# End of the experts: first products of the next model between the last loads, and a padded third tile in retention

## The chip, the core and the metric

One core of a Trainium2 chip runs the whole program in one launch. Its engines work side by side, each on its own list of instructions, strictly in the order of the list: TensorE (PE; the loading of its weights is shown as PEld), VectorE (DVE), ScalarE (ACT), GpSimd (POOL), and SyncE (SP), which here only issues loads and stores. An instruction that has to wait for another engine holds up everything behind it in its list. The metric is the time of one execution in microseconds.

## What is computed

Two small transformer models in a row, on 256 tokens and 16 meta tokens (272 columns), width 1024, float32. The first has one layer: a mixer, then 32 experts in four groups, of which each token uses two. Its output passes a norm and is the input of the second model, whose first layer is retention: four heads, each with q, k, v and a gate from one projection.

```python
u = rmsnorm(h, norm_ffn_g[l]).reshape(b * t, d)
h = h + hier_moe(u, ...).reshape(b, t, d)          # 32 experts, silu(x w1) * (x w3) @ w2
return rmsnorm(h, norm_final_g)[:, N_META:]        # input of the second model
...
proj = hn @ w_in                                   # hn = rmsnorm of it, 1024 -> 6144
q = apply_rope(q, cos, sin); k = apply_rope(k, cos, sin) * (DK ** -0.5) * valid
sc = einsum(q, k) * decay; o = einsum(sc, v)       # per head, by chunks of 64
on = (o - mean) * rsqrt(var + GN_EPS) * gn_g
return (silu(gate) * on) @ w_o
```

## The kernel before

**Wide products.** A weight of the second model is split into a high part (wh, on ScalarE) and a low part (wl, on VectorE), and the input likewise into U's two halves. Each tile of 128 x 128 makes three products of 272 columns (lines 313, 314 and 315). A *block* is 128 outputs; over the 1024 inputs it takes 8 tiles, 24 products. One split covers 8 tiles, one load of 1 MB 16 tiles. A split of a weight writes one of three pairs of buffers; a load goes to one of three buffers named raw.

**Experts.** The 32 experts are done in 8 rounds of 4; a round `g` takes 24 loads of 1 MB (16 for w1 and w3, 8 for w2), 192 in all. I count them from 0 to 191; the last round has 168 to 191, the last eight of which are its w2, in two halves `z` of four. `expert_fetch` issues them on SP (line 1079), into 13 buffers in turn: 3 raw, 6 raw2, 4 raw3. At load 182 it first issues the second model's first load (`second_fetch`, line 1075), which takes a raw buffer too. After the four loads of one half z, ScalarE copies the result (`y`, line 1046), TensorE spreads it back to the tokens (line 1050) and VectorE adds it to the residual `h` (line 1052). `enter` then makes U of h, eight parts of 128 rows in all.

**The handover.** The first four blocks of retention's projection are computed in two steps, because U's second half is ready only after the last load: `begin_first` does inputs 0 to 511 of all four blocks (48 products) just ahead of the last load's products, and `begin_rest` the other 48 behind the last `y`. The input's norm factor isn't known yet: products are made of the input without it, and the factor `row` is multiplied in afterwards (`enter_norms`, two steps, lines 1204 to 1217: a chain of small operations on VectorE, then a product that spreads it over 128 rows, line 1214). retention multiplies the rotary tables by row (`cr`, `sr`, lines 1307 and 1308) and the first four blocks by these (`ro`, lines 1327 to 1331); GpSimd makes q and k of them (`rq`, `rk`, lines 1332 and 1333). Only then is an accumulator free for block 4.

**Retention.** `rot` makes q and k, and the generator `attention` does a head's scores and outputs in steps, one in the middle of each block of the wide products. The 272 keys are tiles of 128, 128 and 16; products with the third tile have 16 columns of weights (scores, line 1347, and transposes, line 1357) or 16 rows (line 1369). `spread` copies a norm factor to all rows; for 272 columns its third product has 16 rows too (line 440).

What decides the order: the lists are made by a scheduler from the order in which the code is written and from what each instruction waits for, so that an instruction can come earlier than the code has it.

Of the kernel before, what the change touches and what calls it, by code (L numbers as in the profile page):

```python
# [16 lines left out]
P = 128  # L17
# [256 lines left out]
class Kern:  # L274
# [58 lines left out]
    def begin_first(self, ws, nkb, cut, xh, xl, cols, then=None, at=()):  # L333
        ps = [self.acc() for _ in range(3)] + [self.att()]
        for i, (p, (c0, n)) in enumerate(zip(ps, cols)):
            self.tiles(ws, p, range(cut), nkb, xh, xl, c0, n)
            if i in at:
                next(then, None)
        self.begun = list(zip(ps, cols))

    def begin_rest(self, ws, nkb, cut, xh, xl, then=None, at=()):
# [500 lines left out]
    def moe(self):  # L842
# [4 lines left out]
        with ExitStack() as ctx:  # L847
# [150 lines left out]
            for g in range(8):  # L998
# [35 lines left out]
                for z in range(2):  # L1034
                    p = self.att()
                    for f in range(4):
                        if g % 2 and j < 3:
                            gather(j + 1, 4 * z + f)
                        if g == 7 and z == 1 and f == 3:
                            self.begin_first(self.ws, KB, 4, self.u2[:, 0], self.u2[:, 1], [(0, T)] * 4)  # L1040
                        w = self.expert_chunk()
                        for e in range(4):
                            mm(p[32 * e:32 * e + 32], ht[:, f * P + e * 32:f * P + e * 32 + 32],  # L1043
                               w[:, 512 * e:512 * e + 512], start=f == 0, stop=f == 3)
                    y = wk.tile([P, 512], F32, name="y")
                    act(y, p, AF.Copy)
                    for b in (0, 2):
# [126 lines left out]
    def enter_start(self):  # L1174
        self.u2 = self.glob.tile([P, 2, KB, T], F32R, name="U")
        self.nc.vector.tensor_copy(self.h[:, :, :NM], self.meta)
        self.split(self.u2[:, 0, :, :NM], self.u2[:, 1, :, :NM], self.meta_t)

# [20 lines left out]
    def enter_norms(self, r1):  # L1199
# [16 lines left out]
        dve.tensor_copy(self.row[:, NM:], p[:, 256:])  # L1216
        dve.tensor_copy(r1, p[:, :256])
# [75 lines left out]
    def retention(self, u):  # L1293
# [4 lines left out]
        with self.tc.tile_pool(name="ret", bufs=1, reuse_waits="tile") as m, \  # L1298
# [6 lines left out]
            cr = m.tile([P, T], F32, name="cr")  # L1305
            sr = m.tile([P, T], F32, name="sr")
            dve.tensor_mul(cr, self.c("c2"), r)
            dve.tensor_mul(sr, self.c("s2"), r)
# [14 lines left out]
            def rot(name):  # L1323
                o = w.tile([P, 2, T], F32, name=name)
# [244 lines left out]
```

## Time and profile before

| | us |
|---|---|
| time, median of 3 runs | 1493.98 (1493.14 to 1494.16) |
| the profiled execution | 1488.68 |
| its span, first to last instruction | 1487.0 |
| TensorE busy in it | 1317.5 (89%) |
| VectorE, ScalarE, GpSimd busy | 722.1, 522.0, 124.4 |
| mean granted clock of TensorE | 0.929 |

The profiled execution is one run, 5.3 us shorter than the median of the others. All rows of the trace are of it, and its times count from the start of the span. A row of busy times is a stretch; in a row of single instructions the first number is its start and the second its length, and "x8" says how many were merged. The text in square brackets is the idle time ahead of it, and what ended it.

### The profile page before, as it was taken

How to read it: one execution, taken by the hardware profiler on the slowest of the kernel's cores; microseconds unless marked ns; L12 is line 12 of the kernel's file. 1: busy time of each engine (PE TensorE's matmuls, PEld its weight loads, DVE VectorE, ACT ScalarE, POOL GpSimd, SP SyncE). 2: the span in 40 equal slices, each digit the busy share in tenths (PEclk: the TensorE clock that was granted, in tenths of full speed). 3: DMA queues.
4: the chain of work that ended last, by engine and by line, in shares of the span. 5: the costliest groups of instructions: out<-in, count | busy, mean ns of one | idle time of the engine just before them, and what ended most of it. 6: DMA issues, size and time to landing. Idle time of an engine off the chain costs nothing.

```text
span 1487.0 us, 23794 instructions
## 1 busy us (share of the span) xinstructions
PE 1317.5 (89%) x9750; PEld 1048.3 (71%) x9750; DVE 722.1 (49%) x1419; ACT 522.0 (35%) x895; POOL 124.4 (8%) x153
## 2 busy tenths in 40 slices
PE   7999997775777667768999999999999999999997
PEld 7898994220221212104899999999999999899996
DVE  7866684110100101002766665766666865766654
ACT  5466651000000000002333443544444554554442
POOL 4010020000000000000122111100000211100001
PEclk9999999887777878769999999999999999999998
DMA  8443677999999999998334334445555433355551
GB/s 309 133 127 112 217 261 300 425 426 425 426 426 426 426 427 426 427 396 359 117 138 143 127 133 155 153 172 171 173 176 184 165 114 124 132 188 183 197 193 63
DMA packets 55553, 359.54 MB, mean 242 GB/s; under 512 B 6416, under 2 KB 7056, under 8 KB 16144
## 3 DMA queue, kind: packets, MB, share of 16 engines
q1 hardware_dynamic: 55440, 357.97, 63.4%
q8 instruction: 78, 1.28, 0.3%
q14 instruction: 35, 0.29, 0.1%
HBM read 356.90 MB, written 1.05 MB: 241 GB/s over the span
## 4 chain that ended last, share of the span: by engine, by line
PE 49%; DMA 22%; DVE 3%; ACT 1%; issue 1%; POOL 0%; SPq 0%; DVEq 0%; ACTq 0%; POOLq 0%
DMA raw<-in_wm 22%; PE acc L313 14%; PE acc L315 14%; PE acc L314 14%; DVE wl L301 1%; ACT wh L300 1%; PE att L440 1%; PE att L1550 0%; PE att L1367 0%; PE att L1343 0%; DVE U L305 0%; PE att L409 0%; PE att L1043 0%; PE att L1369 0%; PE att L1460 0%
## 5 line engine op out<-in xcount | busy, mean ns | idle before, releaser
L313 PE MATMUL acc<-U,wh 128*128 128x272 f32 (+1 forms) x1456 | 423.2, 291 | 11.6 <-ACT U L304 9.2
L314 PE MATMUL acc<-U,wl 128*128 128x272 f32 (+1 forms) x1456 | 416.3, 286 | 1.4 <-DVE wl L301 1.4
L315 PE MATMUL acc<-U,wh 128*128 128x272 f32 (+1 forms) x1456 | 416.6, 287 | 0.4 <-DVE U L305 0.4
L301 DVE TENSOR_TENSOR wl<-raw,wh 128x1024 fp32r<-128x1024 f32 x232 | 285.3, 1230 | 187.3 <-ACT wh L300 186.8
L300 ACT ACTIVATE wh<-raw 128x1024 fp32r<-128x1024 f32 x232 | 245.6, 1060 | 325.2 <-PE acc L315 209.9
L313 PEld LDWEIGHTS acc<-U,wh 128*128 128x128 f32 x1456 | 275.7, 189 | 17.6 <-ACT U L304 10.2
L314 PEld LDWEIGHTS acc<-U,wl 128*128 128x128 f32 x1456 | 276.0, 190 | 2.6 <-DVE wl L301 1.6
L315 PEld LDWEIGHTS acc<-U,wh 128*128 128x128 f32 x1456 | 275.4, 189 | 2.8 <-DVE h L1052 0.8
L1012 PE MATMUL acc<-raw,U 128*32 128x512 f32 x1024 | 185.9, 822 | 86.5 <-DMA raw<-in_wm 81.3
L1012 PEld LDWEIGHTS acc<-raw,U 128*32 128x32 f32 x1024 | 25.0, 124 | 229.8 <-DMA raw<-in_wm 205.2
L1026 DVE TENSOR_TENSOR hid<-hid,acc 128x512 f32<-128x512 f32 x8 | 5.5, 688 | 218.0 <-PE acc L1012 218.0
L315 PE MATMUL acc<-hl,wh 128*128 128x272 f32 (+1 forms) x352 | 99.4, 283 | 0.0
L314 PE MATMUL acc<-hh,wl 128*128 128x272 f32 (+1 forms) x352 | 99.3, 282 | 0.0
L313 PE MATMUL acc<-hh,wh 128*128 128x272 f32 (+1 forms) x352 | 99.1, 281 | 0.0
L1043 PE MATMUL att<-raw,ht 128*32 128x512 f32 x512 | 74.5, 680 | 23.6 <-DMA raw<-in_wm 19.4
L301 DVE TENSOR_TENSOR wl<-rawh,wh 128x512 fp32r<-128x512 f32 x112 | 81.0, 757 | 17.9 <-ACT wh L300 17.8
L1052 DVE TENSOR_TENSOR h<-h,att 128x512 f32<-128x512 f32 x32 | 22.0, 688 | 129.7 <-PE att L1050 129.7
L300 ACT ACTIVATE wh<-rawh 128x512 fp32r<-128x512 f32 x112 | 65.0, 624 | 33.8 <-PE acc L315 20.4
L313 PEld LDWEIGHTS acc<-hh,wh 128*128 128x128 f32 x352 | 66.3, 188 | 0.0
L315 PEld LDWEIGHTS acc<-hl,wh 128*128 128x128 f32 x352 | 66.2, 188 | 0.0
L314 PEld LDWEIGHTS acc<-hh,wl 128*128 128x128 f32 x352 | 66.1, 188 | 0.0
L313 PE MATMUL acc<-yh,wh 128*128 128x272 f32 (+1 forms) x192 | 56.7, 295 | 3.2 <-DVE h L362 3.2
(387 smaller groups left out, 1832.7 us busy)
## 6 DMA issues: line engine op xcount, KB each, us to landing
raw<-in_wm SPq DMA_DIRECT2D x192, 1024.0 KB, 19.6
raw<-in_ws SPq DMA_DIRECT2D x114, 1024.0 KB, 4.9
rawh<-in_ws SPq DMA_DIRECT2D x56, 512.0 KB, 4.0
raw<-in_ws SPq DMA_DIRECT2D x4, 512.0 KB, 18.5
const<-in_const SPq DMA_DIRECT2D x1, 1056.0 KB, 15.3
out<-Q SPq DMA_DIRECT2D x4, 256.0 KB, 2.5
h<-in_xt SPq DMA_DIRECT2D x2, 272.0 KB, 4.8
h<-in_xt SPq DMA_DIRECT2D x1, 544.0 KB, 7.4
```

What stands on the lines that cost most here:

```text
L300: self.nc.scalar.activation(hi, src, AF.Copy)
L301: self.nc.vector.tensor_sub(lo, src, hi.bitcast(F32))
L313: mm(p[:, :n], wh, xh[:, kb, c0:c0 + n], start=kb == first, stop=False)
L314: mm(p[:, :n], wl, xh[:, kb, c0:c0 + n], start=False, stop=False)
L315: mm(p[:, :n], wh, xl[:, kb, c0:c0 + n], start=False, stop=kb == nkb - 1)
L440: self.nc.tensor.matmul(p[:, c:c + m], y[:m, i:i + 1].to_broadcast([m, P]), self.c("ident")[:m, :m], start=True, stop=True)
L1012: mm(p[32 * e:32 * e + 32], XG[:, j % 2, kb, c:c + 32], w[:, 512 * e:512 * e + 512], start=kb == 0, stop=kb == KB - 1)
L1026: dve.tensor_mul(hid, hid, hh[1])
L1043: mm(p[32 * e:32 * e + 32], ht[:, f * P + e * 32:f * P + e * 32 + 32], w[:, 512 * e:512 * e + 512], start=f == 0, stop=f == 3)
L1052: dve.tensor_add(h[:, k:k + 2, NM:], h[:, k:k + 2, NM:], p.rearrange("p (j n) -> p j n", j=2))
```

## The change

- The four first blocks are now one generator (`begin_blocks`), a block a step: one step each ahead of the last three loads' products in the code, and the fourth behind the last y. `begin_rest` has a fifth block (`more`), whose two halves stand around the norm's second step.
- The last ten loads (182 to 191) take the ten buffers raw2 and raw3; the second model's first load is issued behind load 187, when part of the last round's h is done.
- The rotary tables are multiplied by the norm factor in place, straight from the accumulator, and the copies of the factor go to ScalarE.
- k and v get a third tile of 128, cleared on GpSimd behind the 16 keys, and products with it have 128 rows and columns; the third product of `spread` has 128 rows.

```diff
+    def begin_blocks(self, ws, nkb, cut, xh, xl, cols, then=None, at=()):
+        self.begun = []
+        for i, (c0, n) in enumerate(cols):
+            p = self.acc() if i < 3 else self.att()
+            self.begun.append((p, (c0, n)))
+            self.tiles(ws, p, range(cut), nkb, xh, xl, c0, n)
...
+            yield
...
+        if more:
+            p = self.att()
+            self.begun.append((p, more))
+            self.tiles(ws, p, range(nkb // 2), nkb, xh, xl, *more)
+            next(then, None)
+            self.tiles(ws, p, range(nkb // 2, nkb), nkb, xh, xl, *more)
...
-            self.nc.tensor.matmul(p[:, c:c + m], y[:m, i:i + 1].to_broadcast([m, P]), self.c("ident")[:m, :m],
+            self.nc.tensor.matmul(p[:, c:c + m], y[:, i:i + 1].to_broadcast([P, P]), self.c("ident")[:, :m],
...
-                        if g == 7 and z == 1 and f == 3:
-                            self.begin_first(self.ws, KB, 4, self.u2[:, 0], self.u2[:, 1], [(0, T)] * 4)
...
+                        if g == 7 and z == 1 and f == 0:
+                            parts = self.begin_blocks(self.ws, KB, 4, self.u2[:, 0], self.u2[:, 1], [(0, T)] * 4)
+                        if g == 7 and z == 1 and f:
+                            next(parts, None)
...
+                            if k == 6:
+                                next(parts, None)
                             self.enter(k)
                             self.enter(k + 1)
                             if k == 2:
+                                self.second_fetch()
                                 self.ws.split()
                                 self.ws.split()
...
-            self.begin_rest(self.ws, KB, 4, self.u2[:, 0], self.u2[:, 1], self.enter_norms(self.r1), (4, 7))
+            self.begin_rest(self.ws, KB, 4, self.u2[:, 0], self.u2[:, 1], self.enter_norms(self.r1), (4,), (0, T))
...
-        if self.nraw == 192 - 192 % len(self.slots):
-            self.second_fetch()
-        name = self.slots[self.nraw % len(self.slots)]
+        last = self.nraw >= 192 - 192 % len(self.slots)
+        name = self.slots[self.nraw % len(self.slots) + (RAW if last else 0)]
...
-        dve.tensor_copy(self.row[:, NM:], p[:, 256:])
-        dve.tensor_copy(r1, p[:, :256])
+        for x in (self.c("c2"), self.c("s2")):
+            dve.tensor_mul(x[:, NM:], x[:, NM:], p[:, 256:])
+        nc.scalar.copy(self.row[:, NM:], p[:, 256:])
+        nc.scalar.copy(r1, p[:, :256])
...
-            dve.tensor_mul(cr, self.c("c2"), r)
-            dve.tensor_mul(sr, self.c("s2"), r)
+            cr, sr = self.c("c2"), self.c("s2")
...
+                if n > T:
+                    gps.memset(o[:, :, T:], 0.0)
...
-                    mm(p[:16, :64], k[:, d, 256:], q[:, d, 208:], start=d == 0, stop=d == 1)
+                    mm(p[:, :64], k[:, d, 256:], q[:, d, 208:], start=d == 0, stop=d == 1)
...
-                        nc.tensor.transpose(p[:n, b * P:(b + 1) * P], vt[:, b, i * P:i * P + n], ident)
+                        nc.tensor.transpose(p[:, b * P:(b + 1) * P], vt[:, b, i * P:(i + 1) * P], ident)
...
-                    mm(p[:, 208:272], vc[:16, 2, v], sc[:16, 464:], start=False, stop=True)
+                    mm(p[:, 208:272], vc[:, 2, v], sc[:, 464:], start=False, stop=True)
...
-                k = rot("rk")
-                vt = w.tile([P, 4, T], F32, name="vt")
+                k = rot("rk", 3 * P)
+                vt = w.tile([P, 4, 3 * P], F32, name="vt")
+                gps.memset(vt[:, :, T:], 0.0)
```

SP's list at the end of the experts, before, from load 181 on (raw3_5363 is its buffer; in_wm are the experts' weights, in_ws2 the second model's):

```order
L1079 DMA raw3_5363<-in_wm 128x2048
L242 DMA raw_5369<-in_ws2 128x2048
L1079 DMA raw_5371<-in_wm 128x2048
L1079 DMA raw_5377<-in_wm 128x2048
L1079 DMA raw_5400<-in_wm 128x2048
L1079 DMA raw2_5406<-in_wm 128x2048
```

And now:

```order
L1098 DMA raw3_5363<-in_wm 128x2048
L1098 DMA raw2_5369<-in_wm 128x2048
L1098 DMA raw2_5375<-in_wm 128x2048
L1098 DMA raw2_5400<-in_wm 128x2048
L1098 DMA raw2_5406<-in_wm 128x2048
L1098 DMA raw2_5412<-in_wm 128x2048
L1098 DMA raw2_5418<-in_wm 128x2048
L242 DMA raw_5459<-in_ws2 128x2048
L1098 DMA raw3_5470<-in_wm 128x2048
```

The second model's load moved from ahead of load 182 to behind load 187, and load 184 (raw_5400, now raw2_5400) no longer takes a raw buffer.

TensorE's list around the last load's products (raw3_5538 before, raw3_5514 now; att_5489 and att_5551 are the accumulator of the fourth block, S and y the spreading back), before:

```order
L313 MATMUL att_5489<-U_5383,wh_5463 128x272
L314 MATMUL att_5489<-U_5383,wl_5464 128x272
L315 MATMUL att_5489<-U_5383,wh_5463 128x272
L1043 MATMUL att_5467<-raw3_5538,ht_5395 32x512 x4
L1050 MATMUL att_5546<-S_5397,y_5544 128x256 x2
L1050 MATMUL att_5558<-S_5397,y_5544 128x256 x2
L313 MATMUL acc_5486<-U_5383,wh_5577 128x272
```

And now:

```order
L315 MATMUL acc_5520<-U_5381,wh_5465 128x272
L1055 MATMUL att_5469<-raw3_5495,ht_5395 32x512 x4
L1055 MATMUL att_5469<-raw3_5514,ht_5395 32x512 x4
L1066 MATMUL att_5535<-S_5397,y_5533 128x256 x2
L1066 MATMUL att_5547<-S_5397,y_5533 128x256 x2
L313 MATMUL att_5551<-U_5381,wh_5465 128x272
L314 MATMUL att_5551<-U_5381,wl_5466 128x272
```

The fourth block's twelve products moved from ahead of the last load's products to behind those of y.

TensorE's list at the first scores of retention (rq and rk are the first head's q and k, acc_5753 and acc_5755 blocks of its v), before:

```order
L314 MATMUL acc_5753<-U_5383,wl_5755 128x272
L315 MATMUL acc_5753<-U_5383,wh_5754 128x272
L1343 MATMUL att_5772<-rq_5699,rk_5710 128x272 x2
L1343 MATMUL att_5772<-rq_5699,rk_5710 128x192 x2
L1347 MATMUL att_5778<-rq_5699,rk_5710 16x64 x2
L313 MATMUL acc_5753<-U_5383,wh_5754 128x272
```

And now:

```order
L315 MATMUL acc_5755<-U_5381,wh_5756 128x272
L313 MATMUL acc_5785<-U_5381,wh_5786 128x272
L1365 MATMUL att_5804<-rq_5728,rk_5739 128x272 x2
L314 MATMUL acc_5785<-U_5381,wl_5787 128x272
L315 MATMUL acc_5785<-U_5381,wh_5786 128x272
```

The scores moved: before they stood behind 36 products of blocks 4 and 5, now behind all 24 of block 5 and one of block 6.

## Rows read from the trace of the kernel before

**Rows 1.** The chain that ended last: shares of the span by engine.

```profile
PE 49%; DMA 22%; DVE 3%; ACT 1%; issue 1%; POOL 0%; SPq 0%; DVEq 0%; ACTq 0%; POOLq 0%
```

**Rows 2.** Busy time by stretch: us, PE, PEld, DVE, ACT, POOL, clock, DMA, GB/s.

```profile
660.00:664.00 4.00, 1.94 (x8) 0.20 (x8) 0.00 (x0) 0.80 (x1) 0.00 (x0) 0.50 0.99 420
664.00:668.00 4.00, 1.93 (x8) 0.20 (x8) 2.36 (x2) 1.20 (x2) 0.00 (x0) 0.50 0.63 217
676.00:680.00 4.00, 2.25 (x20) 0.32 (x16) 0.00 (x0) 0.00 (x0) 0.00 (x0) 1.00 1.04 436
...
712.00:716.00 4.00, 2.16 (x9) 2.16 (x10) 3.69 (x10) 0.00 (x0) 1.69 (x2) 0.66 0.31 129
720.00:940.00 220.00, 219.32 (x1650) 209.59 (x1649) 143.13 (x264) 92.56 (x143) 42.21 (x47) 1.00 0.41 139
960.00:1140.00 180.00, 180.00 (x1438) 180.00 (x1438) 111.30 (x150) 84.64 (x122) 5.65 (x6) 1.00 0.51 173
```

**Rows 3.** What SP's queue waited for, 640 to 672: total, times, longest.

```profile
SPq L1079 <- DMA raw<-in_ws: 14.2, 1, 14.2
...
SPq L1079 <- DVE wl L301: 3.5, 1, 3.5
```

**Rows 4.** Timeline of the experts' last loads: start, length, engine, operation.

```profile
660.79 1.94 PE L1012 MATMUL acc<-raw,U 128*32 128x512 f32 x8 [0.79 <-DMA raw<-in_wm]
...
665.71 1.93 PE L1012 MATMUL acc<-raw,U 128*32 128x512 f32 x8 [2.98 <-DMA raw<-in_wm]
...
678.90 1.07 PE L1043 MATMUL att<-raw,ht 128*32 128x512 f32 x8 [1.42 <-DMA raw<-in_wm]
680.09 0.60 ACT L1046 ACTIVATE y<-att 128x512 f32<-128x512 f32 x1 [7.45 <-PE att L1043]
...
696.58 1.07 PE L1043 MATMUL att<-raw,ht 128*32 128x512 f32 x8
697.78 0.60 ACT L1046 ACTIVATE y<-att 128x512 f32<-128x512 f32 x1 [5.16 <-PE att L1043]
...
700.88 0.39 PE L313 MATMUL acc<-U,wh 128*128 128x272 f32 x1 [0.46 <-ACT U L304]
```

**Rows 5.** Timeline from the norm's end to the first scores.

```profile
713.84 0.60 PE L313 MATMUL acc<-U,wh 128*128 128x272 f32 x1 [2.25 <-DVE ro L1328]
...
716.73 0.29 PE L313 MATMUL acc<-U,wh 128*128 128x272 f32 x1
...
717.67 1.77 POOL L1333 TENSOR_TENSOR rk<-ro,ro 128x272 f32<-128x272 f32 x1
...
719.73 1.73 PE L1343 MATMUL att<-rq,rk 128*128 128x272 f32 x8
```

**Rows 6.** Timeline of TensorE at small products and at what follows them.

```profile
737.29 0.60 PE L1357 MATMUL att<-const,vt 128*128 128x128 f32 x4
737.65 0.37 PE L313 MATMUL acc<-U,wh 128*128 128x272 f32 x1
...
745.06 0.43 PE L1369 MATMUL att<-sc,vc 16*128 16x64 f32 x2
745.42 0.40 PE L313 MATMUL acc<-U,wh 128*128 128x272 f32 x1
...
954.48 0.92 PE L440 MATMUL att<-const,rs_z 128*128 128x128 f32 x6
955.33 0.39 PE L313 MATMUL acc<-U,wh 128*128 128x272 f32 x1
```

**Rows 7.** Retention's small weight loads by line: busy, mean ns, idle before, releaser.

```profile
L1357 PEld LDWEIGHTS att<-const,vt 128*128 128x128 f32 (+1 forms) x48 | 5.3, 124 | 0.3
...
L1369 PEld LDWEIGHTS att<-sc,vc 16*128 16x128 f32 x32 | 4.7, 182 | 3.6 <-issue 3.6
...
L1347 PEld LDWEIGHTS att<-rq,rk 128*16 128x16 f32 x16 | 0.9, 96 | 0.9 <-issue 0.9
```

**Rows 8.** DMA issues by line: count, KB each, median us to landing.

```profile
raw<-in_wm SPq DMA_DIRECT2D x192, 1024.0 KB, 19.6
```

More of the change, by code (lines that the diff above doesn't have):

```diff
@@ L333, in begin_first @@
     def begin_first(self, ws, nkb, cut, xh, xl, cols, then=None, at=()):
-        ps = [self.acc() for _ in range(3)] + [self.att()]
-        for i, (p, (c0, n)) in enumerate(zip(ps, cols)):
+        for _ in self.begin_blocks(ws, nkb, cut, xh, xl, cols, then, at):
+            pass
+    def begin_blocks(self, ws, nkb, cut, xh, xl, cols, then=None, at=()):
[3 more added lines that the diff above has]
+            self.begun.append((p, (c0, n)))
             self.tiles(ws, p, range(cut), nkb, xh, xl, c0, n)
@@ L338, in begin_first, with begin_rest @@
                 next(then, None)
-        self.begun = list(zip(ps, cols))
-    def begin_rest(self, ws, nkb, cut, xh, xl, then=None, at=()):
+            yield
+    def begin_rest(self, ws, nkb, cut, xh, xl, then=None, at=(), more=None):
         for kb in range(cut, nkb):
@@ L1177, in enter_start @@
         self.split(self.u2[:, 0, :, :NM], self.u2[:, 1, :, :NM], self.meta_t)
+        for x in (self.c("c2"), self.c("s2")):
+            self.nc.vector.tensor_mul(x[:, :NM], x[:, :NM], self.row[:, :NM])
     def enter(self, b):
@@ L1215, in enter_norms @@
                              start=True, stop=True)
-        dve.tensor_copy(self.row[:, NM:], p[:, 256:])
-        dve.tensor_copy(r1, p[:, :256])
+        for x in (self.c("c2"), self.c("s2")):
+            dve.tensor_mul(x[:, NM:], x[:, NM:], p[:, 256:])
+        nc.scalar.copy(self.row[:, NM:], p[:, 256:])
+        nc.scalar.copy(r1, p[:, :256])
     def prep(self, parts, c0):
@@ L1304, in retention @@
             r = self.row
-            cr = m.tile([P, T], F32, name="cr")
-            sr = m.tile([P, T], F32, name="sr")
-            dve.tensor_mul(cr, self.c("c2"), r)
-            dve.tensor_mul(sr, self.c("s2"), r)
+            cr, sr = self.c("c2"), self.c("s2")
             yh = m.tile([P, 16, T], F32R, name="yh")
@@ L1321, in retention, with rot @@
             self.gens.append(residual())
-            def rot(name):
-                o = w.tile([P, 2, T], F32, name=name)
+            def rot(name, n=T):
+                o = w.tile([P, 2, n], F32, name=name)
+                if n > T:
+                    gps.memset(o[:, :, T:], 0.0)
                 p1 = self.dense(ws, KB, uh, ul)
@@ L1331, in rot @@
                 dve.tensor_mul(t[3], p2, cr)
-                gps.tensor_sub(o[:, 0], t[0], t[2])
-                gps.tensor_add(o[:, 1], t[1], t[3])
+                gps.tensor_sub(o[:, 0, :T], t[0], t[2])
+                gps.tensor_add(o[:, 1, :T], t[1], t[3])
                 return o
@@ L1346, in attention @@
                 for d in range(2):
[L1347 to L1348 removed]
+                    mm(p[:, :64], k[:, d, 256:], q[:, d, 208:], start=d == 0, stop=d == 1)
+                dve.tensor_mul(sc[:, 464:], p[:, :64], dret[:, hd, 464:])
                 for _ in range(4):
@@ L1353, in attention @@
                 mu = wk.tile([P, 3], F32, name="mu")
-                for i, n in ((0, P), (1, P), (2, 16)):
+                for i in range(3):
                     p = self.att()
                     for b in range(4):
-                        nc.tensor.transpose(p[:n, b * P:(b + 1) * P], vt[:, b, i * P:i * P + n], ident)
-                    act(vc[:n, i], p[:n], AF.Copy, accum_out=mu[:n, i:i + 1])
-                    dve.tensor_scalar(mu[:n, i:i + 1], mu[:n, i:i + 1], -1.0 / 512, None, op0=ALU.mult)
-                    dve.tensor_scalar(vc[:n, i], vc[:n, i], mu[:n, i:i + 1], None, op0=ALU.add)
+                        nc.tensor.transpose(p[:, b * P:(b + 1) * P], vt[:, b, i * P:(i + 1) * P], ident)
+                    act(vc[:, i], p, AF.Copy, accum_out=mu[:, i:i + 1])
+                    dve.tensor_scalar(mu[:, i:i + 1], mu[:, i:i + 1], -1.0 / 512, None, op0=ALU.mult)
+                    dve.tensor_scalar(vc[:, i], vc[:, i], mu[:, i:i + 1], None, op0=ALU.add)
                     yield
@@ L1387, in retention @@
                 for b in range(4):
-                    dve.tensor_mul(vt[:, b], self.dense(ws, KB, uh, ul), r)
+                    dve.tensor_mul(vt[:, b, :T], self.dense(ws, KB, uh, ul), r)
                 for b in range(4):
```

1 line of the change is left out of this document (removed).

## The prediction

> **What bounds the kernel now.** I read the chain of waits first, then the busy shares by stretch, then what the load queue waited for, then the timeline of the handover from the experts to the second model, and last the small products inside retention. The chain [rows 1] is half TensorE and a fifth DMA. These are two regimes one after the other: to about 700 us the weights of the experts come at 420 GB/s and TensorE waits for each load [rows 2]; from 720 us to the end TensorE itself is the bound: 219.32 of 220 us busy through retention, 180.00 of 180 in the feed-forward, where 1438 matmuls make 0.125 us each [rows 2]. So time saved on TensorE after 720 us comes off the end one for one, and so does any earlier start of that regime; VectorE and ScalarE, with 143 and 93 of 220 us, have room.
>
> The handover between them is not tight. Load 184 of the experts sits in a "raw" buffer that still holds the first weights of the second model; the queue waits 14.2 us for them to arrive and 3.5 us for their split [rows 3], and the 8 loads behind it wait too. The stream falls to 217 GB/s for 4 us [rows 2]. Later, in one stretch, TensorE does the last down-projections and 48 first products; it finishes the last load's products at 697.65 (696.58 + 1.07), and y follows at 697.78 [rows 4]. After that the norm chain and the rotary products hold TensorE until 713.84, and it restarts at the lower of its two clock levels: 0.66 in that window, 12 matmuls in 2.89 us (713.84 to 716.73) [rows 2, 5].
>
> **The change, part by part.**
>
> *Loads.* The last ten loads (182 to 191) go to the ten raw2 and raw3 buffers, and the second model's first load moves behind load 187. Load 182 then needs the buffer of load 172 instead of 169, ten back instead of thirteen. Loads come (665.71 - 660.79) / 2 = 2.46 us apart [rows 4] and land 19.6 us after their issue [rows 8], eight steps; each buffer's products end within 2 us of its landing, so ten steps leave some 3 us spare and the queue shouldn't wait. No other work has to cover this; where the spare is gone, each load is late by what is missing. With the stream whole, load 181's products start at 660.79 as before [rows 4], and load 187 comes six steps later: 660.79 + 6 x 2.46 = 675.55 instead of 678.90 [rows 4]. Term: -3.4 us. The second model's load (seventh step, 678.0) is split then, on ScalarE and VectorE, which wait there anyway; its first products need h from y, which at 680.09 - 3.4 = 676.7 [rows 4] plus some 3 us comes later still. Load 191 lands at the eleventh step, 687.9, before TensorE gets to it. Below nothing this term can't go unless the ten buffers fail; at most it is the bubble's whole lack of bytes, 4 us x (420 - 217) / 420 = 1.9 us, and the resynchronised landings, to 4.5.
>
> *First products by blocks.* Before, all four blocks (48 matmuls) stand ahead of load 191's products; now three, and the fourth behind y. From y to y it took 697.78 - 680.09 = 17.69 us [rows 4]; without 12 matmuls 12 x 0.125 = 1.5 less. Term: -1.5. So y comes at 692.9. Were TensorE not the bound there but load 191, y would come at 689 (another -4); were the products waiting for the late split, the term is nought.
>
> *Behind y.* Before, TensorE went from y to the first product of block 4 in 713.84 - 697.78 = 16.06 us [rows 4, 5]. Now the 12 moved matmuls stand in the gap before 700.88, where it waited for ScalarE's U [rows 4]. Block 4 (24 matmuls) is put in two halves around the norm's spreading product, where TensorE stood still: it restarted only at 713.84 [rows 5]. VectorE loses two copies and two products there and gains two products, but two weight splits instead of one now stand in the norm's chain; these about cancel, and I take the distance from y to the first free accumulator as the same 16 us, with a block more behind it (a us either way). Term: 24 x 0.125 = -3.0. With the holes filled TensorE shouldn't fall to the lower clock: 2.89 - 12 x 0.125 = 1.4; I take -1.2, as some hole stays.
>
> *The new wait.* The first scores now stand 25 matmuls behind the norm's end instead of 36, and need rk, GpSimd's last sum, which ended at 717.67 + 1.77 = 719.44, 5.6 us behind the point where the accumulator came free; the scores started at 719.73 [rows 5]. Now TensorE is there after 25 x 0.125 = 3.1 us, and the second score product needs the sum; the first needs only the other half of rk. Queued behind it on TensorE are all of block 6's products, and the splits that wait for these. Of 5.6 - 3.1 = 2.5 us, 0.6 is the first score product and its switch. Term: +1.9; nought if GpSimd's sum comes in time, 2.5 at worst.
>
> Sum of the handover: -3.4 - 1.5 - 3.0 - 1.2 + 1.9 = -7.2 us.
>
> *Padding.* Sixteen times (4 heads x 4 blocks) a product of 16 rows follows two of 128. Its weight load waits 0.23 us each (3.6 us in 16) [rows 7], and from its start the next wide product comes 0.36 us later (745.06 to 745.42) with two loads; four loads of 128 rows take the same 0.36 (737.29 to 737.65) [rows 6], so two take 0.14: 0.22 saved behind it. Of the wait ahead of it most lies under the product that still runs; I take 0.08. Together 0.30 each, 16 x 0.30 = 4.8 us, with bounds of 0 and 0.45 each. The spreading product of 272 columns has six loads, two of 16 rows, and takes 0.85 us (954.48 to 955.33); six at the rate of the transposes take 0.36 + 2 x 0.11 = 0.58 [rows 6]. Seven of these stand after the experts: 7 x 0.27 = 1.9, bounds 0 and 2.5. The scores' and transposes' third tiles get weight loads of 128 columns for 16: the scores' load takes 96 ns now [rows 7], four a head; at 182 ns this costs 16 x 0.09 = 1.4 at most, and gains 0.9 (its idle) at most; I take nothing. The clears on GpSimd (eight, beside 42 of 220 us busy [rows 2]) hide under it. Sum: -6.7 us.
>
> One rule weighed here. The loads of 16 rows idle 3.6 us in 16, while the transposes' loads, a third of which have 16 columns, idle 0.3 us in 48 [rows 7]. The Trainium skill, TensorEngine Tiling (Array Packing), section Key Properties, says that changing the tiling mode, not just the tile, drains TensorE. The trace agrees for the rows and not for the transposes' columns; by the rule four padded transposes would give 4 x 0.3 = 1.2 us more, 1478.9 in place of 1480.1.
>
> All: -13.9. The profiled execution took 1488.68 us, 1.7 of it outside the span of 1487.0; 1488.68 - 13.9 = 1474.8. The median of the runs is 1493.98, 5.3 above it; I expect the same distance again: 1480.1.
>
> **The rivals.**
>
> A. *Padding is worth nothing*: what follows a small product is the change of product, not its rows. For it: a load of 16 rows and 128 columns takes 182 ns, one of 128 rows and 16 columns 96 [rows 7], so more rows make no load shorter. Against it: the idle before it. Time: 1493.98 - 7.2 = 1486.8. The Trainium skill, TensorE: Matmul & The Clock Gate, section LDWEIGHTS, has this as a rule: a load's time goes by its columns and not by its rows. The trace agrees on the load's own duration; the rule is silent on the wait ahead of it.
>
> B. *The early products bring nothing*: the late split, the wl that stands ahead of U on VectorE, and rk hold TensorE for as long as the load stream gains. For it: each of these is a queue in order. Against it: VectorE is idle at 676 to 680 [rows 2]. Time: 1493.98 - 6.7 = 1487.3.
>
> C. *Slower: TensorE stays at the lower clock from 676 to 708.* Its work there is spread thinner between loads, and where it waited for loads the clock stood at 0.50 (664 to 668) [rows 2]. 120 matmuls at 2.89 / 12 = 0.24 us instead of 0.125 cost 13.8 us, five loads' products at 1.93 instead of 1.07 us [rows 4] cost 4.3: 18.1 - 13.9 = +4.2, time 1498.2. It turns to slower from a low clock over 13.9 / 18.1 = 77% of that stretch. Against it: the clock was 1.00 from 676 on [rows 2], with the same waits. The Trainium skill, TensorE: Matmul & The Clock Gate, section Loop structure matters more than you think, says that matmuls with a DMA wait between them run cold; the trace agrees at 664 and not at 676.
>
> D. *The change doesn't reach the end*: ten buffers are too few, the queue waits again, the bubble only moves, and block 4's place is paid back by rk. Padding then gives half. Time about 1490.6.
>
> **How the numbers follow.** Forecast 0.60, A 0.12, B 0.14, C 0.06, D 0.08. The forecast's own range is 1475.5 (y four us earlier, at load 191) to 1484 (padding at half, rk's wait whole). To leave out no more than two in ten the range goes to 1475 and to 1488, with A and B in it. About 0.2% (3 us) is what a measurement of this kernel can tell from no change. Faster by more than that: the forecast, A, B and half of D, 0.89; within: the other half and a piece of C, 0.06; slower 0.05.
>
> **What would show it.** The load queue's 17.7 us of waits gone and no stretch under 400 GB/s before 690; y of the last experts' product near 692.9; three first blocks before it and the fourth behind; no clock below 1.00 between 690 and 720; a wait of TensorE for rk of up to 2 us; the 16 loads in retention without idle before them, and the same stretch of 220 us shorter by 5. It is wrong if y comes after 696, if the clock falls between 676 and 700, or if the padded product starts no sooner after its neighbour than 0.4 us.

## The result, and the profile after

| | before | after |
|---|---|---|
| time, median of 5 runs each, same chip | 1493.98 us (1489.59 to 1497.24) | 1476.87 us (1476.61 to 1483.05) |
| ratio, 95% interval | | 0.99 (0.9882 to 0.9919) |
| the profiled execution, and its span | 1488.68, 1487.0 | 1476.84, 1475.1 |

The time fell by 17.1 us; 13.9 were forecast, and 1476.87 lies 3.2 below the 1480.1 of the forecast, inside its range. The two traces differ by only 11.84 us. So the trace gained 2 us less than the sum of the terms, and the runs 3 us more. That gap is what many of the experiments went into.

The chain of waits of the kernel after, shares by engine; it answers to [rows 1] and is the same two regimes:

```profile
PE 50%; DMA 21%; DVE 3%; ACT 1%; issue 0%; POOL 0%; SPq 0%; DVEq 0%; ACTq 0%; POOLq 0%
```

Busy time by stretch, after (columns as in [rows 2]; PEclk is the third number from the end, GB/s the last):

```profile
664.00:668.00 4.00, 2.56 (x16) 0.62 (x12) 0.89 (x2) 0.31 (x1) 0.47 (x1) 0.75 1.02 426
668.00:672.00 4.00, 2.24 (x17) 0.31 (x16) 0.00 (x0) 0.60 (x1) 0.00 (x0) 1.00 1.01 422
676.00:680.00 4.00, 1.90 (x12) 1.39 (x9) 2.01 (x3) 2.94 (x6) 0.00 (x0) 0.95 1.03 428
680.00:684.00 4.00, 4.00 (x15) 3.57 (x15) 2.07 (x4) 1.93 (x5) 0.00 (x0) 0.50 1.01 425
684.00:688.00 4.00, 4.00 (x25) 2.15 (x23) 1.15 (x3) 0.78 (x3) 0.00 (x0) 0.69 1.00 412
712.00:716.00 4.00, 2.87 (x20) 2.22 (x18) 3.71 (x7) 1.06 (x1) 2.95 (x3) 1.00 0.00 0
720.00:940.00 220.00, 218.24 (x1687) 215.25 (x1687) 147.88 (x280) 95.53 (x148) 45.88 (x53) 0.99 0.43 147
960.00:1140.00 180.00, 180.00 (x1440) 179.93 (x1439) 112.13 (x158) 82.96 (x119) 6.50 (x12) 1.00 0.51 177
```

The dip to 217 GB/s at 664 us is gone, and so is the low clock at 712. New is the clock of 0.50 (1.2 GHz) at 680 to 684 with TensorE busy throughout: 15 matmuls in 4 us, where 33, of other sizes, fitted at 2.4 GHz in 688 to 692. The 220 us of retention hold 1687 matmuls instead of 1650.

What the load queue waited for, 640 to 672 us, after ([rows 3] before):

```profile
SPq L1098 <- DMA raw<-in_wm: 22.9, 11, 2.1
```

Eleven waits of 2.1 us at most, one a load: that is the pace of the stream, no wait of 14.2.

The timeline of the handover, after (TensorE's rows, then ScalarE's; start, length; [rows 4, 5] before):

```profile
674.98 1.06 PE L1055 MATMUL att<-raw,ht 128*32 128x512 f32 x8 [1.40 <-DMA raw<-in_wm]
676.82 1.13 PE L1066 MATMUL att<-S,y 128*128 128x256 f32 x4 [0.78 <-ACT y L1062]
...
680.44 2.05 PE L1066 MATMUL att<-S,y 128*128 128x256 f32 x4
...
684.19 1.94 PE L1055 MATMUL att<-raw,ht 128*32 128x512 f32 x8
...
692.26 1.92 PE L1055 MATMUL att<-raw,ht 128*32 128x512 f32 x16
...
696.60 0.48 PE L313 MATMUL att<-U,wh 128*128 128x272 f32 x1
...
710.68 0.36 PE L313 MATMUL acc<-U,wh 128*128 128x272 f32 x1
...
714.21 0.73 PE L1365 MATMUL att<-rq,rk 128*128 128x272 f32 x2 [0.16 <-POOL rk L1354]
715.90 0.72 PE L1365 MATMUL att<-rq,rk 128*128 128x272 f32 x2 [0.97 <-POOL rk L1355]
...
676.17 0.60 ACT L1062 ACTIVATE y<-att 128x512 f32<-128x512 f32 x1 [7.43 <-PE att L1055]
694.31 0.60 ACT L1062 ACTIVATE y<-att 128x512 f32<-128x512 f32 x1 [9.53 <-PE att L1055]
```

The first y comes at 676.17, the last at 694.31, and the first product into a free accumulator at 710.68, 16.37 us behind y (16.06 before). Four products that took 1.13 us at 676.82 take 2.05 at 680.44: that is the low clock. The wait for rk is 0.16 + 0.97 = 1.13 us.

The padded products in the timeline, after ([rows 6] before):

```profile
741.78 0.49 PE L1390 MATMUL att<-sc,vc 128*128 128x192 f32 x2
742.10 0.33 PE L1391 MATMUL att<-sc,vc 128*128 128x64 f32 x2
742.24 0.37 PE L313 MATMUL acc<-U,wh 128*128 128x272 f32 x1
...
941.33 0.73 PE L454 MATMUL att<-const,rs_z 128*128 128x128 f32 x6
941.92 0.37 PE L313 MATMUL acc<-U,wh 128*128 128x272 f32 x1
```

The next wide product starts 0.14 us behind the start of the third tile's (0.36 before), and 0.59 behind the spreading product's (0.85 before). And their weight loads in 720 to 940 us (by line; busy, mean ns, idle before; [rows 7] before):

```profile
L1379 PEld LDWEIGHTS att<-const,vt 128*128 128x128 f32 x48 | 5.7, 141 | 0.0
L1391 PEld LDWEIGHTS att<-sc,vc 128*128 128x128 f32 x32 | 5.6, 190 | 0.0
```

3.6 us of idle in 32 loads are now none, though each load is 8 ns longer.

### The profile page after: what moved, and what is told of

It reads as the page before. It is cut to its first block, busy times and chain, and to the rows that moved or that the text cites. A ratio compares the mean times of both kernels' runs of the same rounds, so it can differ in the third digit from the quotient of the medians.

```text
span 1475.1 us, 23814 instructions
## 1 busy us (share of the span) xinstructions
PE 1302.9 (88%) x9750; PEld 1048.9 (71%) x9750; DVE 719.5 (49%) x1419; ACT 522.5 (35%) x897; POOL 126.8 (9%) x161
## 3 DMA queue, kind: packets, MB, share of 16 engines
HBM read 356.90 MB, written 1.05 MB: 243 GB/s over the span
## 4 chain that ended last, share of the span: by engine, by line
PE 50%; DMA 21%; DVE 3%; ACT 1%; issue 0%; POOL 0%; SPq 0%; DVEq 0%; ACTq 0%; POOLq 0%
DMA raw<-in_wm 21%; PE acc L313 15%; PE acc L315 14%; PE acc L314 14%; DVE wl L301 1%; PE att L1055 1%; PE att L1573 1%; PE att L1389 0%; ACT wh L300 0%; PE att L1365 0%; PE att L423 0%; DVE U L305 0%; PE att L454 0%; PE att L1483 0%; PE att L1379 0%
## 5 line engine op out<-in xcount | busy, mean ns | idle before, releaser
L1026 PE MATMUL acc<-raw,U 128*32 128x512 f32 x1024 | 181.9, 805 | 88.8 <-DMA raw<-in_wm 83.7
L1055 PE MATMUL att<-raw,ht 128*32 128x512 f32 x512 | 70.1, 647 | 26.7 <-DMA raw<-in_wm 22.6
L1055 PEld LDWEIGHTS att<-raw,ht 128*32 128x32 f32 x512 | 12.1, 113 | 67.4 <-DMA raw<-in_wm 50.3
## 6 DMA issues: line engine op xcount, KB each, us to landing
raw<-in_ws SPq DMA_DIRECT2D x4, 512.0 KB, 16.7
```

The costliest lines, as they stand in the source:

```text
L1026: mm(p[32 * e:32 * e + 32], XG[:, j % 2, kb, c:c + 32], w[:, 512 * e:512 * e + 512], start=kb == 0, stop=kb == KB - 1)
```

## The experiments

Three distances in each trace separate the stages: from the issue of load 180 to the first y of the last round, from there to the last y, and from that to the 1000th product of line 315, counted from 0 (near 950 us, behind retention). All in us, read from the starts of single instructions. The expectations count loads from 1, and "load 181" there is this load 180. A star: a chance dip of the clock near the 970th product is in the last number, 1.53 us (14.54 instead of 13.01 us from the 955th to the 980th). Ahead of load 180 the change touches only two spreading products (at 24 and 574 us); its issue comes at 637.96 to 643.40 us in the fourteen traces, before the change at 638.46 and 640.20. So the spans of two traces can differ by some us for what stands ahead of the change, and the distances leave that out.

| kernel | load 180 to first y | y to y | y to 1000th |
|---|---|---|---|
| before | 41.63 | 17.69 | 262.43* |
| before, again | 41.52 | 20.87 | 261.14 |
| padding only | 41.49 | 20.87 | 253.90 |
| loads only | 39.05 | 21.02 | 261.89 |
| handover only | 38.15 | 18.14 | 259.71* |
| after | 38.18 | 18.14 | 252.44* |
| two_before | 38.37 | 14.95 | 250.94 |
| one_before | 38.21 | 22.64 | 250.93 |
| four_before | 39.05 | 21.02 | 250.64 |
| no_fifth | 38.20 | 18.13 | 255.59* |
| third_64 | 38.20 | 22.67 | 258.28 |
| keep_busy | 40.87 | 14.95 | 252.44* |
| busy_long | 39.49 | 14.94 | 250.94 |
| busy_four | 38.88 | 16.79 | 252.20* |

**The kernel before, once more.** No edit.

> The kernel before, unchanged, profiled and timed once more. Theory (single events make the difference between executions): the profiled time falls anywhere between 1488 and 1498 us, the ratio to the runs of the kernel before is 1.000 within 0.002, and TensorE's products stand at the same times to 0.3 us up to some place, where one trace loses 1 to 5 us at a wait with a low granted clock behind it. Rival (the prediction's step: a profiled execution is 5.3 us shorter than the median): the profiled time is 1488 to 1489 us again and the median of the runs 1494.

Median 1495.01 us, ratio 1.0014 (0.9996 to 1.0032); profiled 1492.21. The theory holds for the times, and the rival falls. The two traces part early, though, and not at one place: load 180 is issued 1.7 us later here. Busy time by stretch of the first trace of before and then of this one:

```profile
684.00:688.00 4.00, 4.00 (x24) 2.06 (x23) 2.05 (x6) 1.68 (x5) 0.00 (x0) 1.00 0.99 416
688.00:692.00 4.00, 4.00 (x31) 3.15 (x32) 0.00 (x0) 0.44 (x1) 0.00 (x0) 1.00 1.02 363
```

```profile
684.00:688.00 4.00, 3.18 (x14) 2.83 (x14) 1.31 (x4) 1.52 (x4) 0.00 (x0) 0.69 1.01 424
688.00:692.00 4.00, 4.00 (x15) 1.29 (x14) 1.56 (x5) 1.52 (x4) 0.00 (x0) 0.50 1.00 369
```

The same program at the same place, once with a clock of 1.00 and once with 0.69 and 0.50: y to y took 17.69 and 20.87 us. The trace that the prediction was made from had no fall there; this one and that of the padding alone had it, with 20.87 in both.

**Padding alone, handover alone, loads alone.** Each is a part of the change, put into the kernel before (padding, loads) or left when the padding is taken out of the kernel after (handover):

```diff
-                    mm(p[:, 208:272], vc[:16, 2, v], sc[:16, 464:], start=False, stop=True)
+                    mm(p[:, 208:272], vc[:, 2, v], sc[:, 464:], start=False, stop=True)
...
-        if self.nraw == 192 - 192 % len(self.slots):
-            self.second_fetch()
-        name = self.slots[self.nraw % len(self.slots)]
+        last = self.nraw >= 192 - 192 % len(self.slots)
+        name = self.slots[self.nraw % len(self.slots) + (RAW if last else 0)]
```

> The kernel before with the padding alone: third tile of scores, transposes, products and the spreading product at 128 rows. Theory (from the trace of the changed kernel, where the stretch from the neighbour's start to the second wide product behind is 0.512 us instead of 0.848): 16 x 0.336 + 7 x 0.27 + 4 x 0.08 = 7.6 us less, all of it between 720 and 1180 us, nothing before; median 1486.4. The prediction's size: 6.7 us less, 1487.3. Rival A (padding is worth nothing): 0, 1494.

1486.08 us, ratio 0.9954 (0.9935 to 0.9973), to 1493.34 of the 32 runs of before: 7.3 us less. From y to the 1000th product it takes 253.90 instead of 261.14, 7.24 us less, and the stages ahead are as before. Rival A falls. The weight loads of the third tile's product in this kernel:

```profile
L1371 PEld LDWEIGHTS att<-sc,vc 128*128 128x128 f32 x32 | 5.6, 190 | 0.0
```

> The changed kernel with the third tile and the spreading product at 16 rows as before: the handover alone. Theory (both parts add): the products behind the first attention stand 6.4 us earlier than in the kernel before, y of the last load at 694.3, median 1487.6. The prediction's size: 7.2 us earlier, 1486.8. Rival B (early products bring nothing): 0 to 1 us, 1494. TensorE's granted clock between 680 and 688 us: 0.5 to 0.7 again if the pace of the loads brings it down, 1.0 if it was chance.

1485.37 us, ratio 0.9941 (0.9921 to 0.9960): 8.0 us less. Rival B falls. The last y stands 56.29 us behind the issue of load 180, as after (56.32), and behind y it takes 259.71 - 1.53 = 258.2 us, 3.0 less than in "before, again". The clock fell (0.64 and 0.51 in the two stretches of 684 to 692), so the changed kernel's fall was not of the padding. Both parts add behind y: 7.24 + 3.0 = 10.2, and after against "before, again" 261.14 - (252.44 - 1.53) = 10.2.

> The kernel before with the loads moved alone (ten raw2 and raw3 buffers for the last ten loads, the second model's first load behind load 187); first products, norm and padding as before. Theory 1 (the load stream sets the handover): first y at 676.2 instead of 680.1, last y and all behind 3.4 to 3.9 us earlier, median 1490.3. Theory 2 (TensorE takes the gain back): first y at 676.2, but TensorE falls to a granted clock of 0.5 to 0.7 at 680 to 688 us, 3 us of longer products, and the last y and all behind come at most 1 us earlier, median 1493 to 1494.

1489.13 us, ratio 0.9969 (0.9951 to 0.9987). The products of load 187 and the y's of this kernel, from its timeline:

```profile
674.95 1.93 PE L1043 MATMUL att<-raw,ht 128*32 128x512 f32 x8 [1.39 <-DMA raw<-in_wm]
677.01 0.60 ACT L1046 ACTIVATE y<-att 128x512 f32<-128x512 f32 x1 [8.73 <-PE att L1043]
698.03 0.60 ACT L1046 ACTIVATE y<-att 128x512 f32<-128x512 f32 x1 [11.30 <-PE att L1043]
```

Load 187 lands 36.95 us behind the issue of load 180, as in after, and 40.27 in "before, again": 3.3 us are gained. The first y is only 2.5 us nearer, because the clock had already fallen (0.50 in 676 to 680): the products of load 187 took 1.93 us, where they take 1.06 in after. The clock stays low until 688, as theory 2 has it (y to y 21.02). But two of the three traces with the order of before fall as well (20.87), so little was paid that it doesn't pay too, and the median went theory 1's way, 4.2 us down.

**More products ahead of the fall.** In the kernel after, the products of w2's first half are issued again into a spare accumulator:

```diff
+                        if g == 7 and z == 0:
+                            idle = self.att()
+                            for e in range(4 if f < 3 else 2):
+                                mm(idle[32 * e:32 * e + 32], ht[:, f * P + e * 32:f * P + e * 32 + 32],
+                                   w[:, 512 * e:512 * e + 512], start=True, stop=True)
```

> The changed kernel with 14 more expert products into an accumulator that nobody reads, behind the first half's down-projections of the last expert block (4, 4, 4 and 2 of them), where TensorE waits 1.4 us for each load. Theory (TensorE falls to its lower level at 680 to 688 us because it waits between loads, and that costs 3 us): granted clock 1.00 from 676 to 690, the last y 53.3 us after the issue of load 181 instead of 56.3, everything behind it 3 us earlier, median 1473.9. Rival 1 (the fall comes all the same or comes later): y at 56.3, 1476.9. Rival 2 (load 191 sets y): clock 1.00, but y no earlier than 55, 1475.5.

1476.58 us, ratio 0.9880 (0.9858 to 0.9902): no gain. By stretch:

```profile
668.00:672.00 4.00, 2.45 (x16) 1.06 (x16) 0.89 (x2) 0.91 (x2) 0.00 (x0) 0.50 1.01 422
672.00:676.00 4.00, 4.00 (x24) 0.84 (x20) 0.00 (x0) 0.00 (x0) 0.00 (x0) 0.50 1.02 424
```

A fall came earlier, from 666 us on. The first additional product starts at 672.7, so it can't have brought it: up to there TensorE's list is that of after. The additional products then ran at 1.2 GHz ahead of the first y, which came 2.7 us later (40.87). Behind it the clock was 1.00 and y to y 14.95. What the products cost ahead of the first y (2.7) and what the clock gave behind it (3.2) nearly cancel: no gain in time, as in rival 1, but the theory is right on what the fall costs.

**No fifth block.** The norm's second step stands in the last quarter of the four blocks again:

```diff
-            self.begin_rest(..., self.enter_norms(self.r1), (4,), (0, T))
+            self.begin_rest(..., self.enter_norms(self.r1), (4, 7))
```

> The changed kernel without the fifth block of first products in the norm's wait (it comes later with the other blocks; the norm's last step stands behind the last quarter of the four blocks as before). Theory (its 24 products fill holes of TensorE): 24 x 0.125 = 3.0 us later behind the norm, 1479.9, with a hole of some 3 us before the restart. With a low clock behind the hole, as in the kernel before, up to 1.2 more. Rival (the norm ends earlier by what the block takes, since its spreading product no longer waits for 12 products): 0 to 1 us later, 1477 to 1478.

1480.88 us, ratio 0.9910 (0.9892 to 0.9929). TensorE's waits in the norm, from its timeline:

```profile
710.91 1.13 PE L1235 MATMUL att<-const,rs_z 128*128 128x128 f32 x8 [1.62 <-DVE rs_z L400]
713.67 0.57 PE L313 MATMUL acc<-U,wh 128*128 128x272 f32 x1 [1.63 <-ACT s L1240]
```

Two holes of together 3.25 us are back, with a granted clock of 0.68 in 712 to 716, and y to the 1000th product takes 255.59 instead of 252.44: 3.15 us. The theory holds.

**Where the four blocks stand.** All four ahead of the last y, in the kernel after:

```diff
                             next(parts, None)
+                            if f == 3:
+                                next(parts, None)
                     y = wk.tile([P, 512], F32, name="y")
```

> The changed kernel with all four blocks of first products ahead of the last y, as before, and none directly behind it. Theory (behind y the chain ScalarE, VectorE, norm sets the time): the last y 12 x 0.125 = 1.5 us later and everything behind it 1.5 us later, 1478.4. Rival (TensorE itself sets the time behind y, 27.84 of 30 us busy): y 1.5 us later, but the first product behind the norm at the same time, 1476.9.

1479.24 us, ratio 0.9898 (0.9879 to 0.9918). Behind y nothing is won back (250.64, after 250.9 without its dip): the chain behind y sets the time there, as the theory says. The 21.02 us to y are 2.9 more than after and hold a longer fall, which begins ahead of the first y as in "loads only" (39.05 to it in both), so this trace doesn't give the block's own price.

Then two blocks or one ahead, with the rest behind y in the code:

```diff
-                        if g == 7 and z == 1 and f:
+                        if g == 7 and z == 1 and f > 1:
```

> The changed kernel with two of the four blocks of first products ahead of the last y and two directly behind it (the changed kernel has three and one). Theory (behind y the chain from y over ScalarE and VectorE to the norm sets the time, and products ahead of y run partly at the lower clock level): the last y 1.5 to 3.7 us sooner after the issue of load 181 than 56.3, what stands behind y unchanged to 0.5 us, so the end 1.5 to 3.5 us earlier, 1473.4 to 1475.4. Rival (TensorE itself is the bound behind y by now): y earlier, but the products behind the first attention come after y by as much later, 1476.9.

> As the kernel with two blocks ahead of the last y, with one ahead and three behind. Theory (chain behind y): y a further 1.5 to 3 us earlier unless load 191 (landing 49 us after the issue of load 181) sets it: its products, 1.1 us, and y then come at 51 at the earliest; behind y TensorE has 36 products, 4.5 us, to do where the chain waits some 2 us for U and 3 us later for the norm, so 0 to 2 us come back; median 1472 to 1476. Rival (TensorE is the bound behind y): all comes back, 1476.9 or later.

Neither could be tested. The scheduler lifts the blocks to the same place: in both traces 36 first products run between the two y's as after, and all instructions of all engines stand in the order of the kernel after, but for two neighbours on TensorE at 571 us in two_before. So these are two more executions of that order, with medians of 1476.59 (0.9881, 0.9857 to 0.9904) and 1478.12 (0.9888, 0.9871 to 0.9906). ScalarE's y's of the kernel named two_before and a stretch of it, and the same of one_before:

```profile
677.34 0.60 ACT L1062 ACTIVATE y<-att 128x512 f32<-128x512 f32 x1 [6.54 <-PE att L1055]
692.29 0.60 ACT L1062 ACTIVATE y<-att 128x512 f32<-128x512 f32 x1 [7.68 <-PE att L1055]
```

```profile
684.00:688.00 4.00, 4.00 (x35) 3.35 (x34) 0.98 (x3) 0.61 (x2) 0.00 (x0) 1.00 1.01 419
```

```profile
677.61 0.60 ACT L1062 ACTIVATE y<-att 128x512 f32<-128x512 f32 x1 [6.90 <-PE att L1055]
700.25 0.60 ACT L1062 ACTIVATE y<-att 128x512 f32<-128x512 f32 x1 [13.88 <-PE att L1055]
```

```profile
684.00:688.00 4.00, 4.00 (x18) 2.08 (x17) 2.62 (x4) 1.52 (x4) 0.00 (x0) 0.50 1.01 421
692.00:696.00 4.00, 4.00 (x18) 2.09 (x17) 0.07 (x2) 0.00 (x0) 0.00 (x0) 0.50 0.86 361
```

One order of instructions, and y to y took 14.95, 18.14 and 22.64 us: no fall, one from 680 to 687 us (after), one from 680 to 697 (one_before). Whether the clock falls there and for how long differs from execution to execution, and it is worth up to 7.7 us. What decides it is open.

**A TensorE that is busy throughout.** The products of the last round's 16 up loads and four first down loads twice, those of the last of these by half (the edit of "keep_busy", in both loops):

> The changed kernel with every expert product of the last block repeated into an accumulator that nobody reads, for its 16 up loads and the first four down loads, so that TensorE works 2.1 of every 2.48 us from about 618 us on. Theory (a TensorE that works without long waits keeps the upper level, and the fall at 680 to 688 us costs 3 us): granted clock 1.00 from about 640 to 690, first y at 38 to 38.5 us after the issue of load 181 as in the changed kernel, last y at 53.3 instead of 56.3, median 1473.9. Rival 1 (the extra products themselves bring the level down, as in the run with fewer of them, where it fell to 0.50 at 668 to 676): clock 0.5 to 0.7 before 680 us, first y 1 to 3 us later, last y no earlier than 55.8, 1476.5 or later.

1478.72 us, ratio 0.9893 (0.9875 to 0.9912). Two stretches of it, and the products of load 187:

```profile
656.00:664.00 8.00, 6.03 (x52) 1.25 (x48) 0.00 (x0) 0.00 (x0) 0.00 (x0) 1.00 1.01 423
680.00:692.00 12.00, 10.68 (x80) 8.00 (x82) 5.30 (x10) 5.05 (x10) 0.00 (x0) 1.00 1.01 423
```

```profile
677.85 1.06 PE L1061 MATMUL att<-raw,ht 128*32 128x512 f32 x8 [1.85 <-DMA raw<-in_wm]
```

The clock stood at 1.00 from 640 to 700, y to y 14.94. So the theory holds for the clock, and the fall costs 18.14 - 14.94 = 3.2 us. Chance isn't quite excluded: of the eight traces with the loads moved and no product repeated, one (two_before) had no fall between the y's either; of the three with repeated products none had one. (The Trainium skill, TensorE: Matmul & The Clock Gate, section Loop structure matters more than you think, says that matmuls with long waits for DMA between them run cold. The traces agree in part: in after the clock was 1.00 in 668 to 672 us with TensorE busy 2.24 of 4 us.)

The first y comes 1.3 us later (39.49), and not for the products: load 187, issued 17.24 us behind load 180 (17.26 in after), landed at 38.25 instead of 36.95, and y follows the landing by 1.24 us in both. Why it landed late no run shows (in busy_four it landed at 37.64). The median is no better than after; the 1.9 us that are left of the gain are less than the interval can tell.

**The blocks at the full clock.** The same, with all four blocks ahead of the last y:

> The kernel with the last block's expert products repeated (as in the run of that name, where the granted clock stayed at 1.00 and the last y came 14.94 us after the first), with all four blocks of first products ahead of the last y. Theory (TensorE sets the time from y to y at the full clock): 12 x 0.125 = 1.5 us for the products and some 0.25 for one more change between them and the 32-column expert products: last y 16.7 us after the first, all behind 1.5 to 2 us later than in that run. Rival 1 (load 191 sets the last y): 14.95 us. Rival 2 (four blocks ahead cost what the two traces at full clock differ by, 17.69 - 14.95): 17.7 us. If the level falls in spite of the repeated products: about 21 us, as in the other two kernels with four blocks ahead.

1479.15 us, ratio 0.9899 (0.9877 to 0.9921).

```profile
684.00:700.00 16.00, 14.08 (x102) 9.91 (x103) 5.16 (x10) 5.32 (x12) 0.00 (x0) 1.00 0.97 406
```

The clock held, and y to y took 16.79 us: theory (16.7). The fourth block ahead of y costs 16.79 - 14.94 = 1.85 us, and load 191, which landed 6.0 us ahead of y, isn't what sets it.

**Another size of the padding.** Third tile of 64, the spreading product's last piece of 32 rows:

```diff
-                    mm(p[:, 208:272], vc[:, 2, v], sc[:, 464:], start=False, stop=True)
+                    mm(p[:, 208:272], vc[:64, 2, v], sc[:64, 464:], start=False, stop=True)
```

> The changed kernel with the third tile at 64 instead of 128 (scores' columns, transposes' columns, rows of the product) and the spreading product's last piece at 32 rows. Theory (any change of the number of rows costs a drain, whatever the number): the product's stretch 0.75 to 0.85 us instead of 0.512, the spreading product's 0.9 to 0.98 instead of 0.707, scores and transposes as with 128 columns to 0.05 us; together 16 x 0.3 + 7 x 0.25 = 6.5 us, 1483.4. Rival (the cost goes with the rows left out, 64 of 112 and 96 of 112): 0.34 x 16 x 0.57 + 0.27 x 7 x 0.86 = 4.7 us, 1481.6. Rival A (nothing): 1476.9.

1481.15 us, ratio 0.9913 (0.9891 to 0.9934), too wide to tell the two sizes apart; the rows do. Weight loads, and the timeline of one product:

```profile
L1392 PEld LDWEIGHTS att<-sc,vc 64*128 64x128 f32 x32 | 4.7, 184 | 3.6 <-issue 3.6
L1380 PEld LDWEIGHTS att<-const,vt 128*64 128x64 f32 x16 | 1.8, 111 | 0.0
```

```profile
750.22 0.49 PE L1391 MATMUL att<-sc,vc 128*128 128x192 f32 x2
750.64 0.43 PE L1392 MATMUL att<-sc,vc 64*128 64x64 f32 x2
751.00 0.40 PE L313 MATMUL acc<-U,wh 128*128 128x272 f32 x1
```

64 rows idle 3.6 us in 32 loads, exactly what 16 rows did [rows 7], and the next wide product comes 0.36 us behind the start, as with 16 [rows 6]. The spreading product with 32 rows takes 0.98 us from its neighbour's start to the first wide product behind; 16 rows 0.98, 128 rows 0.71. For these numbers of rows the price is the same, so it is that of a change in their number. (The Trainium skill, TensorEngine Tiling (Array Packing), section Key Properties, has TensorE drain when the tiling mode changes. For rows these traces agree, with the idle of 3.6 us.) For columns it is mixed: the transposes' 16 loads of 64 columns idle 0.0 us like those of 128, those of 16 columns 0.3, and no transpose is faster by its padding; but the scores' third tile takes 0.86 us with 64 columns, 0.81 with 16 and 0.73 with 128.

## Why the prediction came out as it did

The direction and the range were right, and so were the mechanisms of the parts as far as the runs separate them; the forecast was 3.2 us too high. Distances at like clock, by its terms:

- **Loads, -3.4.** Measured 41.5 to 38.2 = -3.3. The 14.2 us wait is gone and no stretch before 692 is below 412 GB/s. Right. Moved alone, they land 3.3 earlier too, and 0.86 of it goes to a clock that fell ahead of the first y.
- **First products by blocks, -1.5: mis-sized.** At the full clock y to y fell from 17.69 to 14.95, with the shorter fall from 20.87 to 18.14: -2.7 both times. 12 x 0.125 left out what comes with them, 1.85 in all (busy_four). The other 0.9, between 17.69 and busy_four's 16.79, has no experiment; the 32-column expert products between the y's stand in five groups in before, in four in busy_four (in three in after).
- **Behind y, -3.0 - 1.2 + 1.9 = -2.3.** Measured -3.0 (261.14 to 258.2). The fifth block is worth 3.15 with the low clock behind the hole, less than the 4.2 of the first two terms; the wait for rk is 1.13 instead of 1.9. That makes 2.0; the other 1.0 no run separates.
- **Padding, -6.7: a little too small.** ([rows 7] has two loads to each of the sixteen products, 32 in all; the 0.23 us of the prediction are a product's, not a load's.) The sixteen products give 0.848 - 0.512 = 0.336 us each (0.30 forecast), so 5.4; the seven spreading products 0.27 each, so 1.9, as forecast; the scores' four 0.08 each, 0.3 (nothing forecast). That is -7.6. The transposes gained nothing, so the rule on the tiling mode was rightly kept out of the sum for them, and rival A (a load's time goes by its columns) described the load, not the idle ahead of it.
- **Given back later: not foreseen.** At 1273 us (1287 before) TensorE waits 2.67 us for VectorE in either kernel. Busy time behind that wait, of before, after, and the kernel with 64 rows:

```profile
1287.00:1291.00 4.00, 3.38 (x27) 3.25 (x27) 3.99 (x9) 3.40 (x9) 2.28 (x3) 1.00 0.43 178
```

```profile
1273.00:1277.00 4.00, 3.40 (x16) 3.40 (x17) 3.32 (x8) 3.42 (x9) 2.25 (x3) 0.57 0.43 180
```

```profile
1288.00:1292.00 4.00, 3.58 (x29) 3.38 (x29) 3.99 (x8) 3.68 (x9) 2.35 (x3) 1.00 0.36 150
```

All nine traces with 128 rows have the low clock there and need 19.95 to 20.16 us from the 1755th to the 1795th product of line 315; the five with 16 or 64 rows have none and need 18.94 to 18.98. It takes 1.1 us back from the padding. The code there is the same in both; why it comes with the padding is open.

Sum: -3.3 - 2.7 - 3.0 - 7.6 + 1.1 = -15.5. The timed difference is -17.1, or -16.4 between all 32 runs of before in the first set (1493.34) and the 16 executions of the order after (median 1476.9). The interval is 2.8 us to either side, so the 0.9 to 1.6 that are left can't be told from nothing.

**The step that failed** is the last one: "I expect the same distance again." The 5.3 us between the profiled execution and the median of before were no constant. That execution had no fall of the clock between the y's, where the other two traces with the order of before lose 3.2 us, and it issued load 180 at 638.46 us, 1.0 sooner than the median of the fourteen traces. The traced execution of after has such a fall, and the slower of the two rhythms told below, 1.05; its early part was short as well (637.99), and the dip near the 970th product is in both. So trace against trace shows -11.84, less than the change is worth, and the distance of after is 0.03 us. The forecast of -13.9 from a lucky trace and the 5.3 added to it missed by 1476.84 - 1474.8 = +2.0 and 0.03 - 5.3 = -5.3, together the -3.2 by which the time came out below it. That the two misses partly cancel is luck.

**Rival C** (TensorE stays at the lower clock) did occur, in part: 0.50 and 0.69 from 680 to 688, against the forecast's own sign ("if the clock falls between 676 and 700"). It didn't make the kernel slower than before, which falls at the same place in two traces of three that have its order. The prediction took one clean trace of that stretch for its nature. A, B and D fell with the parts run alone; y at 694.31 stayed below the bound of 696.

## What to carry to other kernels

Before a term rests on the granted clock of one stretch, take a second trace of the same kernel: here one order of instructions took 14.95, 18.14 or 22.64 us between the same two points. Split the trace into distances between fixed instructions and compare these; sums over the span mix the change with such falls. Small products amid wide ones did best here with the full 128 rows: 16 rows and 64 rows alike cost 0.34 us each time.

## What the runs showed of the hardware that was not expected

- All three kernels with repeated products had no fall of the clock between the y's. In busy_long they begin at 632 us, with the clock at 1.00, and it stood there through to 700. In keep_busy they begin at 672.7, with the clock at 0.50 since 668, ran at 0.50 themselves, and it was 1.00 from 680 on.
- Near 1300 to 1410 us the same products of 256 columns run in one of two rhythms: starts 0.113 to 0.120 us apart, mean 0.1167, in ten traces, or 0.116 to 0.119, mean 0.1178, in four (handover only, loads only, after, two_before), the granted clock 1.00 in both. Over the 1000 products it makes 1.05 us. The order of instructions doesn't decide it (two_before has the slower, one_before the quicker); what does is open.
